# The second expert's weight loads take their number from the ranking, and the ranking stands ahead of the last table of slots

## The chip, the cores and the metric

The kernel runs on one core of one Trainium2 chip. The metric is the device time of one execution in microseconds (us), the median of several. Three executions of the kernel before took 1479.09, 1485.01 and 1486.35 us; their median is 1485.01 us. Another execution, taken with the profiler, lasted 1480.72 us, and its trace is what the sections below read.

## The reference

One decoder layer on 512 tokens of width 1024, in float32. A mixer (gated DeltaNet heads and sliding-window attention, one output projection) comes first, then a mixture of 32 experts of which each token takes 4. Cut to the second half, with its names:

```python
x = x + gate1 * (mixed @ w_out)
h = rmsnorm(x, norm2_w) * (1.0 + scale2) + shift2
logits = h @ w_router + b_router
top_val, top_idx = lax.top_k(logits, 4)
gates = jax.nn.softmax(top_val, axis=-1)
# for each token and each of its four experts e:
hu = h @ w_up[e] + b_up[e]
x_glu = jnp.minimum(hu[:, :1024], 7.0)
x_lin = jnp.clip(hu[:, 1024:], -7.0, 7.0)
act = x_glu * jax.nn.sigmoid(1.702 * x_glu) * (x_lin + 1.0)
out[token] += gates[token, e] * (act @ w_down[e] + b_down[e])
x = x + gate2 * out
```

An expert has 8 MB of `w_up` and 4 MB of `w_down`; all 32 are read, 384 MB in all.

## The kernel before

**The two stages.** The first stage (some 430 us) computes the mixer, the output projection in four tiles of 128 tokens, and for each tile its routing. The second runs through the 32 experts one after the other, in an order by rank: the experts are sorted by their number of tokens, and the program says which rank comes when and how many tokens a rank may hold. Which expert has a rank is known only at run time, from the ranking; only the expert at the first place (`ORDER[0]`) is fixed in the program. Its 12 weights of 1 MB (8 of `w_up`, 4 of `w_down`) are loaded during the first stage. The second expert is the first whose weights need the ranking.

**The routing of a tile** (`route`) is a chain over VectorE (DVE), TensorE (PE) and ScalarE (ACT): the residual `y` is added up (L1168, L1172), scaled (L1279), transposed (L1283), multiplied by the router (L1299 to L1306), and VectorE finds the four experts (L1311 to L1317, ending in the tile's counts `ohs`, L1316). TensorE then numbers the token within each expert (L1321, L1322), VectorE works out slot numbers (L1325 to L1331), and the table of slots is made: VectorE writes payload and selection (L1183, L1184, four L1192), TensorE multiplies them (L1196, four of them) and VectorE adds the product to `ten` (L1342).

**The ranking** (`ranks`) adds the counts of the four tiles on TensorE (L1504, L1506), compares each expert's count with all others on VectorE (L1508 to L1517, ending in a permutation), and multiplies the permutation on TensorE (L1521, L1522). ScalarE writes the result to `eri` (L1524): the expert number of each rank. `places` multiplies the finished `ten` by the permutation (L1535) and VectorE writes `gi` (L1537), the token numbers of each expert's slots.

**What sets the order.** In the first stage the instructions of all engines stand in the order that a planner (`Flow`) chooses while the program is built: every step is announced with an engine and a cost, and of the steps that can start at nearly the same time the one with the smallest priority number goes first. `PR["rt"]` is 4, so `ranks` is added with 3.9 and the routing of tile i with 4 - 0.2 i; the projection's end (`out_end`) and `finish` stand at 3. Each engine then runs its instructions strictly in that order.

**The start of the second stage.** SyncE's queue (SP) issues all weight loads. GpSimd (POOL) clears a tile `xg` (L1697) and gathers an expert's tokens into it by an indirect DMA (L1698) that reads `gi`; TensorE transposes them (L1711) and starts the up product (L1760). In the kernel before, POOL copies the second expert's number out of `eri` into a one-element tile `second` (L1904), and `behind` puts this copy after the issue of the first gather in POOL's order. SP reads `second` and issues the second expert's loads (L1654). There are 16 places of 1 MB for weights: the first expert holds 12, so the second expert's fifth load waits until TensorE is through with the first expert's first weight. After its sixth load (`THEN1`) SP issues the bias rows of both first experts (L1640); VectorE spreads them (L1720) before it can use any up product.

Of the kernel before, what the change touches and what calls it, by code (L numbers as in the profile page):

```python
# [12 lines left out]
I32 = mybir.dt.int32  # L13
# [12 lines left out]
NE = 32  # L26
# [12 lines left out]
PR = {"swa": 1, "conv": 5, "cend": 4, "in": 4, "late": 1, "z": 2, "load": 1, "yS": 7, "fin": 3, "rt": 4, "yT": 3, "rec": 1, "oout": 2}  # L39
# [10 lines left out]
ORDER = []  # L50
# [133 lines left out]
def layer_kernel(ctx: ExitStack, tc: tile.TileContext, A, out, probe=None):  # L184
    nc = tc.nc
    V, S, G, TE = nc.vector, nc.scalar, nc.gpsimd, nc.tensor
# [109 lines left out]
    def behind(late, early):  # L296

        tc.add_manual_dep(late.ins, early.ins.name,
                          mybir.DependencyInfo(mybir.DependencyClass.NoSync, mybir.DependencyReason.DATA), reason="order")
# [1197 lines left out]
    def ranks():  # L1497
        yield [("chosen", 2), ("oT", 7)]
        yield "N", 0.0, "d", "d"
        pa, pb = bank("d", "ps_cnt"), bank("d", "ps_cnt")  # L1500
        for i in range(NT):
            yield [("chosen", i)]
            yield "P", 0.2
            TE.matmul(pa[:, 0:NE], lhsT=bc(one, [P, P]), rhs=ohs[:, i], start=(i == 0), stop=(i == NT - 1))  # L1504
            for j in range(P // NE):
                TE.matmul(pb[NE * j:NE * j + NE, 0:1], lhsT=ohs[:, i], rhs=one, start=(i == 0), stop=(i == NT - 1))  # L1506
        yield "V", 0.4
        V.scalar_tensor_tensor(kr, pa[:, 0:NE], float(NE), C("KROW"), op0=OP.mult, op1=OP.add)  # L1508
        V.tensor_copy(ec[:, 1:2], pb[:, 0:1])
        V.scalar_tensor_tensor(ec[:, 0:1], ec[:, 1:2], float(NE), C("KCOL"), op0=OP.mult, op1=OP.add)  # L1510
        flow.give("d", "d")
        yield "V", 0.6
        V.tensor_scalar(kr, kr, ec[:, 0:1], None, op0=OP.is_gt)
        V.tensor_reduce(ec[:, 2:3], kr, axis=AX.X, op=OP.add)

        for c in range(2):
            V.tensor_scalar(ex[:, 1 + c], C("IOTA", 0, NE), ec[:, 2:3], C("ISC", c, c + 1), op0=OP.is_equal, op1=OP.mult)  # L1517
        flow.mark("perm")
        yield "P", 0.3, "d"
        pe = bank("d", "ps_er")  # L1520
        TE.matmul(pe[:NE, 0:NE], lhsT=bc(C("PIDX")[:NE], [NE, NE]), rhs=perm[:NE], start=True, stop=True)  # L1521
        TE.matmul(pe[:NE, NE:2 * NE], lhsT=bc(ec[:NE, 1:2], [NE, NE]), rhs=perm[:NE], start=True, stop=True)  # L1522
        yield "S", 0.5
        S.copy(eri, pe[:NE, 0:NE])  # L1524
        S.copy(cnti, pe[:NE, NE:2 * NE])
        S.copy(cnt[:NE], pe[:NE, NE:2 * NE])
        flow.give("d")
# [32 lines left out]
    with tc.manual_schedule(engines={nc.vector.engine, nc.scalar.engine, nc.tensor.engine, nc.gpsimd.engine, nc.sync.engine}):  # L1560
        columns(rows2, 32, 51)
        for i in range(NT):
            (V.tensor_copy if i % 2 else S.copy)(swt[i // 2][:, i % 2, 0:512], tq[i])
        for i in range(2):
            (V.tensor_copy if i % 2 else S.copy)(swt[i][:, :, 512:768], tkv[i].rearrange("p (i n) -> p i n", n=256))

        def chain(*tasks):
            for t in tasks:
                yield from t

        def swa():
            flow.add(PR["swa"], swa_norms())
            for i in range(NT):
                flow.add(PR["swa"], swa_heads(i))
                for kv in range(2):
                    flow.add(PR["swa"], swa_weights(i, kv))
                    flow.add(PR["swa"] - 1, swa_values(i, kv))
            yield [("norms",)]

        order = [(n, p, c0 + 256 * p) for p in range(2) for n, c0 in (("k", 512), ("q", 0), ("v", 1024))]  # L1580
        flow.add(1, gates())
        wins[512, 0] = wins[512, 1] = w0s
        for hf in range(2):
            flow.mark("win", 512, hf)
        flow.taken.update({"x": 2, "r": 1})
        flow.free["V"] = 1.9
        flow.add(0, chain(*(win(c0) for c0 in [c for _, _, c in order][1:] + [1536, 1536 + 256])))
        flow.add(PR["conv"], chain(*(conv(p, n, c0, PR["cend"]) for n, p, c0 in order)))
        for p in range(2):
            for f in (lengths, decay, turned, inverse, levels):  # L1590
                flow.add(PR["in"] + (f is levels), f(p))
        flow.add(PR["swa"], swa())
        flow.add(1, late_loads())
        flow.add(PR["late"], chain(*(late(r) for r in range(2, 6))))
        flow.add(PR["z"], chain(*(gate(p, PR["z"]) for p in range(2))))
        flow.add(PR["load"], loads())
        flow.add(PR["rec"], recur())
        for i in range(NT):
            flow.add(PR["yS"], out_swa(i))
            flow.add(PR["yT"], out_delta(i))  # L1600
            flow.add(PR["rt"] - 0.2 * i, route(i))
            if i < NT - 1:
                flow.add(PR["fin"], finish(i))
        flow.add(PR["rt"], router_bias())
        flow.add(PR["rt"] - 0.1, ranks())
        flow.add(0, places())
        flow.run()
    early.close()
# [265 lines left out]
        G.dma_start(lstd, lst)  # L1874

    down_of = {0: ahead[1]}
    second = const.tile([1, 1], I32, name="second")

    def fetch_up(q):

        r = ORDER[q]
        e = nc.sync.value_load(second if q == 1 else eri[0:1, r:r + 1], min_val=0, max_val=NE - 1)

        def then():
            for p in range(q) if q == 1 else ():
                load_bias(ORDER[p], NB[ORDER[p]], bias[p % 2])
            load_bias(e, NB[r], bias[q % 2])

        ws = weights_of(e)
        wu = load_up(ws[0], then, THEN if q > 1 else THEN1)  # L1890
        if q > 1:
            down_of[q - 1] = load_down(state["dn"])
        state["dn"] = ws[1]
        return wu
# [5 lines left out]
    overflow = overflow_list()  # L1900
    with tc.manual_schedule(engines={nc.sync.engine, nc.tensor.engine, nc.vector.engine, nc.scalar.engine}):
        xs = {0: rows_of(0)}

        behind(G.tensor_copy(second, eri[0:1, ORDER[1]:ORDER[1] + 1]), state["gather"])  # L1904
        ups = {0: ahead[0], 1: fetch_up(1)}
        xs[1] = rows_of(1)
        xT = {0: turn(xs.pop(0))}
        for d in stores[-2:]:
            behind(d, state["turned", 1])
        bbs = {0: spread_bias(NB[ORDER[0]], bias[0])}  # L1910
        acts, pend, last = {}, [], {}
        for q in range(NE + 1):
            if q < NE:
                r = ORDER[q]
                last[q] = None
                if len(units(NB[r])) > 1:
                    last[q] = units(NB[r])[-1], TE.value_load(cnti[0:1, r:r + 1], min_val=0, max_val=T)

                def turn_acts():
                    for p, u, l in pend:  # L1920
                        acts.setdefault(p, {})[u] = turn_act(u, l)
                    pend.clear()

                def turn_next():
                    if q + 1 < NE:
                        xT[q + 1] = turn(xs.pop(q + 1))
                    if q + 2 < NE:
                        xs[q + 2] = rows_of(q + 2)

                if 1 < q + 1 < NE:  # L1930
                    ups[q + 1] = fetch_up(q + 1)
                elif q + 1 == NE:
                    down_of[q] = load_down(state["dn"])
                for z, us in enumerate(passes(NB[r])):
                    pu = up_pass(us, ups[q], xT[q], {3: [turn_acts], 5: [turn_next] if z == 0 else []}, last[q])
                    for u in us:
                        pend.append((q, u, swiglu(u, pu[u], bbs[q])))
                xT.pop(q), ups.pop(q), bbs.pop(q)
            else:
                turn_acts()  # L1940

            if q >= OVQ:
                next(overflow, None)
            if q:
                r = ORDER[q - 1]
                us = units(NB[r])
                py = down(us, down_of.pop(q - 1), acts.pop(q - 1), last.pop(q - 1))
                for u in us:
                    put(u, py[u], si[u[1]][:, u[0] // 64, r:r + 1], sg[u[1]][:, u[0] // 64, r:r + 1])
            if q >= OVQ:  # L1950
                next(overflow, None)
            if q + 1 < NE:
                bbs[q + 1] = spread_bias(NB[ORDER[q + 1]], bias[(q + 1) % 2])
# [47 lines left out]
```

## Time and profile before

| | kernel before |
|---|---|
| median of three runs | 1485.01 us |
| the profiled execution: its time / its span | 1480.72 us / 1478.9 us |
| TensorE, VectorE, ScalarE, GpSimd busy | 1381.5, 563.8, 237.8, 261.1 us |
| weight loads of the experts | 384 of 1 MB |
| bytes moved by DMA | 476.16 MB |

All times below count from the span's start; the profiled execution is 1.8 us longer than its span. A "timeline" row gives the start, the length, the engine, the line, the operation with the tiles it writes and reads, its size and number, and in brackets how long the engine stood idle before it and what ended that. SPq is SyncE's queue, which issues DMAs; such a row's length is the issue alone, and where several issues are merged in one row, the time from the first to the last.

### The profile page before, as it was taken

Reading aid. Unit: us, or ns where it says so; the run is one execution under the profiler, and the core shown is the slowest. Engines: PE = TensorE matmul, PEld = TensorE weight load, DVE = VectorE, ACT = ScalarE, POOL = GpSimd, SP = SyncE. Lnnn points to the kernel's source line nnn. Section 1 sums busy time; section 2 is a strip of 40 time slices with the busy share of each in tenths; the row PEclk is TensorE's granted clock in tenths of the full one; section 3 lists DMA queues with packets and bytes.
Section 4 is the critical chain, followed back from the end, with each engine's and each line's share of the span. In section 5 each row is a group of like instructions: output and inputs, shape, how many; then the busy total and the mean of one; then the engine's idle time right before and its main releaser. Section 6 shows DMA issues by size and latency. Waiting matters only on the chain. (4 is left out here: it accounts for less than half of the span.)

```text
span 1478.9 us, 22303 instructions
## 1 busy us (share of the span) xinstructions
PE 1381.5 (93%) x8586; PEld 601.3 (41%) x8586; DVE 563.8 (38%) x1247; ACT 237.8 (16%) x542; POOL 261.1 (18%) x216
## 2 busy tenths in 40 slices
PE   4999999999879999979999999999999999999974
PEld 3766666765443333322333333333333333343311
DVE  6965567566853222212221231223321323232310
ACT  4354354442211000000000000000000000010000
POOL 2213133202331111101011101102110112211110
PEclk9999999999969999999999999999999999999976
DMA  9655300256349999999999999999998999999995
GB/s 302 212 200 204 113 29 30 58 214 277 116 152 407 409 387 402 396 391 412 411 412 400 379 419 394 384 409 393 410 367 349 403 348 404 393 418 415 414 415 229
DMA packets 104980, 476.16 MB, mean 322 GB/s; under 512 B 13992, under 2 KB 39556, under 8 KB 55714
## 3 DMA queue, kind: packets, MB, share of 16 engines
q1 hardware_dynamic: 91842, 453.16, 77.4%
q0 software_dynamic: 11952, 18.75, 5.5%
q10 hardware_dynamic: 1072, 2.70, 0.5%
q8 instruction: 75, 1.23, 0.3%
q14 instruction: 39, 0.32, 0.1%
HBM read 464.14 MB, written 17.22 MB: 325 GB/s over the span
## 5 line engine op out<-in xcount | busy, mean ns | idle before, releaser
L1760 PE MATMUL ps_up<-we,xTe 128*64 128x512 f32 (+1 forms) x3040 | 622.2, 607 | 21.2 <-DMA we<-in_w_up_dram 16.8
L1760 PEld LDWEIGHTS ps_up<-we,xTe 128*64 128x64 f32 (+1 forms) x3040 | 188.5, 132 | 394.2 <-issue 336.8
L1797 PE MATMUL ps_dn<-we,aT 128*64 128x512 f32 (+1 forms) x1848 | 316.0, 534 | 19.7 <-DMA we<-in_w_down_dram 10.9
L1797 PEld LDWEIGHTS ps_dn<-we,aT 128*64 128x64 f32 (+1 forms) x1848 | 103.7, 129 | 232.2 <-issue 187.2
L1805 POOL DMA_INDIRECT out_dram<-yv,si x52 | 81.7, 1571 | 649.7 <-DVE yv L1804 464.9
L1712 DVE COPY xTe<-ps_xTe 128x256 f32<-128x256 f32 (+3 forms) x35 | 17.5, 501 | 307.4 <-PE ps_xTe L1711 307.4
L1785 ACT COPY aT<-ps_aT 128x512 f32<-128x512 f32 (+1 forms) x52 | 26.0, 530 | 512.5 <-PE ps_aT L1783 509.1
L1769 DVE TENSOR_TENSOR hu<-ps_up,bb 128x512 f32<-128x512 f32 (+1 forms) x52 | 32.1, 617 | 198.8 <-PE ps_up L1760 198.8
L1804 DVE SCALAR_TENSOR_TENSOR yv<-ps_dn,sg,g2p 128x512 f32<-128x512 f32 x38 | 28.5, 751 | 188.3 <-PE ps_dn L1797 187.4
L1771 ACT ACTIVATE hu<-hu 128x512 f32<-128x512 f32 (+1 forms) x52 | 29.8, 573 | 269.4 <-DVE hu L1770 269.4
L1697 POOL MEMSET xg<- 64x1024 f32 (+3 forms) x35 | 37.2, 1084 | 186.0 <-PE ps_xTe L1711 185.8
L317 PE MATMUL ps_ch<-hhi,wih 128*128 128x512 f32 x128 | 58.5, 457 | 0.0
L317 PE MATMUL ps_ch<-hl,wih 128*128 128x512 f32 x128 | 50.8, 397 | 0.0
L317 PE MATMUL ps_ch<-hhi,wl 128*128 128x512 f32 x128 | 50.5, 395 | 0.0
L1720 DVE STREAM_SHUFFLE bb<-bias 128x1024 f32<-128x1024 f32 (+1 forms) x44 | 48.8, 1137 | 0.1
L1712 ACT COPY xTe<-ps_xTe 128x256 f32<-128x256 f32 (+3 forms) x35 | 15.1, 433 | 163.4 <-PE ps_xTe L1711 163.4
L1698 POOL DMA_INDIRECT xg<-h2d,gi x35 | 35.7, 1021 | 16.1 <-POOL xg L1697 8.1
L1711 PEld LDWEIGHTS ps_xTe<-cst,xg 64*128 64x128 f32 (+3 forms) x280 | 24.1, 142 | 32.3 <-issue 23.1
L1783 PEld LDWEIGHTS ps_aT<-cst,act 128*128 128x128 f32 x180 | 24.3, 208 | 28.6 <-issue 25.7
L1711 PE MATMUL ps_xTe<-cst,xg 64*128 64x64 f32 (+3 forms) x280 | 30.1, 249 | 5.1 <-DMA xg<-h2d,gi 2.2
L317 PEld LDWEIGHTS ps_ch<-hhi,wih 128*128 128x128 f32 x128 | 24.2, 189 | 23.2 <-issue 18.0
L1142 PE MATMUL ps_y<-wos,oS 128*128 128x512 f32 x64 | 33.3, 613 | 0.0
(392 smaller groups left out, 1389.0 us busy)
## 6 DMA issues: line engine op xcount, KB each, us to landing
we<-in_w_up_dram SPq DMA_DIRECT2D x256, 1024.0 KB
we<-in_w_down_dram SPq DMA_DIRECT2D x128, 1024.0 KB
wa<-in_w_ada_dram SPq DMA_DIRECT2D x16, 512.0 KB
wi<-in_w_in_dram SPq DMA_DIRECT2D x8, 1024.0 KB
wl<-in_w_ada_dram SPq DMA_DIRECT2D x12, 512.0 KB
oS<-in_w_ada_dram SPq DMA_DIRECT2D x10, 512.0 KB
LL<-in_w_ada_dram SPq DMA_DIRECT2D x10, 512.0 KB
wt<-in_w_in_dram SPq DMA_DIRECT2D x4, 776.0 KB
```

Of the source, the lines that this page charges most:

```text
L317: TE.matmul(acc, lhsT=w[a], rhs=x_[b], start=start and q == 0, stop=stop and q == 2)
L1142: TE.matmul(a, lhsT=oS[:, j, P * i:P * i + P], rhs=wo[j][:, 512 * hf:512 * hf + 512], start=(j == 0), stop=(j == 3))
L1697: G.memset(xg[:rows_], 0.0)
L1698: state["gather"] = G.indirect_dma_start(out=xg[:rows_], out_offset=None, in_=h2d, in_offset=bass.IndirectOffsetOnAxis(ap=gidx(g)[:rows_], ...
L1711: TE.transpose(pt[:, k, :rows_], xg[:rows_, 512 * hf + P * k:512 * hf + P * k + P], ident[:rows_, :rows_])
L1712: state["turned", hf] = (S.copy if hf else V.tensor_copy)(xt_[:, 4 * hf:4 * hf + 4, :rows_], pt[:, :, :rows_])
L1720: V.stream_shuffle(bbs[w].rearrange("p h n -> p (h n)"), b[w], [0] * 32)
L1760: TE.matmul(t[w * j:w * j + w], lhsT=lhsT, rhs=rhs, start=(k == 0), stop=(k == KT - 1))
L1769: V.tensor_tensor(g, pg, bbs[w][:, 0], op=OP.add)
L1771: S.activation(sgm, g, AF.Sigmoid, scale=1.702)
L1797: TE.matmul(py[u][w * j:w * j + w, 0:m], lhsT=aT[u][:, kt % nf, w * (kt // nf):w * (kt // nf) + w], rhs=wd[kt][:, m * j:m * j + m], start= ...
L1805: G.indirect_dma_start(out=outv[u[1]], out_offset=bass.IndirectOffsetOnAxis(ap=sidx, axis=0), in_=yv, in_offset=None, compute_op=OP.add, b ...
```

## The change

Two edits. The second expert's loads read their number from `eri` itself, as those of all later experts do: the tile `second`, POOL's copy and its place behind the first gather are gone. And `ranks` is added to the planner with priority 3 in place of 3.9.

```diff
-        flow.add(PR["rt"] - 0.1, ranks())
+        flow.add(PR["rt"] - 1, ranks())
...
-    second = const.tile([1, 1], I32, name="second")
...
-        e = nc.sync.value_load(second if q == 1 else eri[0:1, r:r + 1], min_val=0, max_val=NE - 1)
+        e = nc.sync.value_load(eri[0:1, r:r + 1], min_val=0, max_val=NE - 1)
...
-        behind(G.tensor_copy(second, eri[0:1, ORDER[1]:ORDER[1] + 1]), state["gather"])
```

The new priority changes the planner's order over some 30 us at the end of the first stage. Three places matter.

VectorE, the last tile, from its slot numbers to the sum of its gates. L1183 to L1192 are the table, L1513 to L1517 the ranking's second half. Before:

```order
L1331 TENSOR_SCALAR slots<-si_3884,cse 128x4
L1508 SCALAR_TENSOR_TENSOR ex<-ps_cnt,cse 128x32
L1509 COPY ec<-ps_cnt 128x1
L1510 SCALAR_TENSOR_TENSOR ec<-ec,cse 128x1
L1183 TENSOR_TENSOR rt<-kS,slots 128x4x32
L1184 TENSOR_TENSOR rt<-kS,slots 128x4x32
L1192 TENSOR_SCALAR room<-cst,slots 128x256 x4
L1513 TENSOR_SCALAR ex<-ex,ec 128x32
L1514 TENSOR_REDUCE ec<-ex 128x1
L1517 TENSOR_SCALAR ex<-cst,ec,cse 128x32 x2
L1338 TENSOR_REDUCE sums<-rt 128x32
```

The same place of the changed kernel:

```order
L1331 TENSOR_SCALAR slots<-si_3882,cse 128x4
L1373 TENSOR_TENSOR bt<-ps_bd,gm 128x512
L1513 TENSOR_SCALAR ex<-ex,ec 128x32
L1514 TENSOR_REDUCE ec<-ex 128x1
L1517 TENSOR_SCALAR ex<-cst,ec,cse 128x32 x2
L1183 TENSOR_TENSOR rt<-kS,slots 128x4x32
L1184 TENSOR_TENSOR rt<-kS,slots 128x4x32
L1192 TENSOR_SCALAR room<-cst,slots 128x256 x4
L1338 TENSOR_REDUCE sums<-rt 128x32
```

The ranking's second half now stands ahead of the table, and so does a product of the third tile's `finish` (L1373) that stood before the choice; L1508 to L1510 moved ahead of L1325, further up.

TensorE, the last tile, from its logits to the product that yields `eri`. Before:

```order
L1306 MATMUL ps_rt<-cst,rt 128x32 x2
L1321 MATMUL ps_rt<-sums,one 128x32 x3
L1322 MATMUL ps_rt<-sums,cse 128x32
L1504 MATMUL ps_cnt<-sums,one 128x32
L1506 MATMUL ps_cnt<-one,sums 32x1 x4
L1196 MATMUL ps_rt<-room,rt 64x256 x4
L1521 MATMUL ps_er<-ex,cst 32x32
```

The same place of the changed kernel:

```order
L1306 MATMUL ps_rt<-cst,rt 128x32 x2
L1504 MATMUL ps_cnt<-sums,one 128x32
L1506 MATMUL ps_cnt<-one,sums 32x1 x4
L1321 MATMUL ps_rt<-sums,one 128x32 x3
L1322 MATMUL ps_rt<-sums,cse 128x32
L1370 MATMUL ps_bd<-bdh,fin 128x512
L1196 MATMUL ps_rt<-room,rt 64x256 x4
L1521 MATMUL ps_er<-ex,cst 32x32
```

The last tile's count now stands ahead of its numbering, and L1521 still stands behind the table's four products.

TensorE, some 15 us earlier, around the third tile's table and the last tile's projection (L1161) and transposes (L1283). Before:

```order
L1161 MATMUL ps_y<-wod,oT 128x512
L1196 MATMUL ps_rt<-room,rt 64x256 x4
L1504 MATMUL ps_cnt<-sums,one 128x32
L1506 MATMUL ps_cnt<-one,sums 32x1 x4
L1161 MATMUL ps_y<-wod,oT 128x512
L1504 MATMUL ps_cnt<-sums,one 128x32
L1506 MATMUL ps_cnt<-one,sums 32x1 x4
L1161 MATMUL ps_y<-wod,oT 128x512
L1283 MATMUL ps_h2T<-cst,h_3811 128x128 x4
```

The same place of the changed kernel:

```order
L1504 MATMUL ps_cnt<-sums,one 128x32
L1506 MATMUL ps_cnt<-one,sums 32x1 x4
L1161 MATMUL ps_y<-wod,oT 128x512
L1283 MATMUL ps_h2T<-cst,h_3800 128x128 x4
L1161 MATMUL ps_y<-wod,oT 128x512
L1321 MATMUL ps_rt<-sums,one 128x32 x2
L1322 MATMUL ps_rt<-sums,cse 128x32
L1196 MATMUL ps_rt<-room,rt 64x256 x4
L1283 MATMUL ps_h2T<-cst,h_3800 128x128 x4
```

The third tile's numbering (L1321, L1322) and table (L1196) moved behind the projection's last products; before, they stood ahead of them.

## Rows read from the trace of the kernel before

**Rows 1.** Windows: us, busy per engine (instructions), clock, DMA share, GB/s.
```profile
420.00:431.50 11.50, 8.13 (x75) 5.87 (x75) 7.74 (x35) 1.49 (x8) 4.21 (x6) 0.50 0.10 27
431.50:441.00 9.50, 7.23 (x25) 3.00 (x24) 3.04 (x5) 0.58 (x1) 7.03 (x9) 0.62 0.89 275
460.00:1440.00 980.00, 947.57 (x5135) 328.77 (x5131) 263.22 (x530) 70.34 (x136) 139.25 (x113) 0.99 1.01 398
```

**Rows 2.** Waits of SyncE's queue: us in total, times, longest.
```profile
SPq L1882 <- POOL second L1904: 25.8, 1, 25.8
```

**Rows 3.** Timeline, from the ranking's result to the second expert's first load.
```profile
426.75 0.17 ACT L1524 CAST eri<-ps_er 32x32 int32<-32x32 f32 x1 [6.20 <-PE ps_er L1522]
429.13 1.10 POOL L1698 DMA_INDIRECT xg<-h2d,gi  x1 [7.12 <-issue]
430.23 0.18 POOL L1904 COPY second<-eri 1x1 int32<-1x1 int32 x1
431.47 0.37 SPq L1654 DMA_DIRECT2D we<-in_w_up_dram  x1
```

**Rows 4.** Timeline, last tile, VectorE and TensorE, from the choice to the ranking.
```profile
418.11 1.49 PE L1321 MATMUL ps_rt<-sums,one 128*128 128x32 f32 x6 [0.36 <-DVE rt L1311]
419.69 0.37 DVE L1316 TENSOR_REDUCE sums<-kS 128x32 f32<-128x128 f32 x1
420.17 1.85 POOL L1697 MEMSET xg<- 128x1024 f32 x2
420.56 0.61 PE L1504 MATMUL ps_cnt<-sums,one 128*128 128x32 f32 x2
420.78 1.26 DVE L1326 TENSOR_SCALAR slots<-rt 128x4 f32<-128x4 f32 x1
422.10 0.29 DVE L1328 TENSOR_REDUCE slots<-rt 128x4 f32<-128x128 f32 x1
423.73 1.13 DVE L1192 TENSOR_SCALAR room<-cst,slots 128x256 f32<-128x256 f32 x4
424.13 2.23 PE L1196 MATMUL ps_rt<-room,rt 128*64 128x256 f32 x8 [2.74 <-DVE room L1192]
424.78 0.23 DVE L1513 TENSOR_SCALAR ex<-ex,ec 128x32 f32<-128x32 f32 x1
425.27 0.51 DVE L1517 TENSOR_SCALAR ex<-cst,ec,cse 128x32 f32<-128x32 f32 x2
426.29 0.31 PE L1521 MATMUL ps_er<-ex,cst 32*32 32x32 f32 x2
```

**Rows 5.** Timeline, third tile's table and last projection.
```profile
401.91 1.02 PE L1161 MATMUL ps_y<-wod,oT 128*128 128x512 f32 x2
402.77 0.30 PE L1504 MATMUL ps_cnt<-sums,one 128*128 128x32 f32 x2
406.25 1.50 PE L1196 MATMUL ps_rt<-room,rt 128*64 128x256 f32 x8 [1.95 <-DVE room L1192]
412.45 0.69 DVE L1279 TENSOR_TENSOR h<-y,gm 128x512 f32<-128x512 f32 x1
```

**Rows 6.** Gathers (L1698): the first, the third, all 35, from issue to landing.
```profile
DMA to landing us min/median/max: 4.8/4.8/4.8
...
DMA to landing us min/median/max: 12.4/12.4/12.4
...
DMA to landing us min/median/max: 4.8/8.5/12.4
```

**Rows 7.** Timeline, the first expert's start.
```profile
435.85 5.09 PE L1760 MATMUL ps_up<-we,xTe 128*64 128x512 f32 x16
440.98 0.33 SPq L1654 DMA_DIRECT2D we<-in_w_up_dram  x1
457.10 0.01 DVE L1720 LOAD_MASK_SELECT bb<-bias  x1 [21.30 <-DMA bias<-in_b_up_dram]
458.77 7.07 PE L1760 MATMUL ps_up<-we,xTe 128*64 128x512 f32 x24 [2.37 <-DVE xTe L1712]
```

## The prediction

> **What bounds the kernel now.** I read the windows first, since the two stages have different limits. From 460 to 1440 us the DMA engines have a share of 1.01 at 398 GB/s, while TensorE is busy 947.57 of 980 us, so 32.4 us of it are idle [rows 1]. This stretch is bound by the stream of expert weights: it ends earlier only if the stream starts earlier or has fewer gaps. Before it, from 420 to 431.5, the DMA share is 0.10 at 27 GB/s, and from 431.5 to 441 it is 0.89 at 275 GB/s [rows 1]: the stream has not begun, then it ramps. The waits of SyncE's queue say why: once, for 25.8 us, it waits for `second` [rows 2]. So a microsecond by which the second expert's first load comes earlier is worth up to one at the end, and no more than the idle DMA time of that place.
>
> **What is removed.** The number stands in `eri` at 426.75 + 0.17 = 426.92. POOL issues the first gather at 429.13, copies from 430.23 to 430.41, and the first load is issued at 431.47 [rows 3]. The detour costs 430.41 - 426.92 = 3.49 us; the 1.06 us from number to issue stay. With `eri` where it is, the first load would come at 427.98, and 3.49 us is the gain at most from this edit.
>
> **What is moved, on the way to `eri`.** Two terms, with opposite signs.
>
> First, how early the last tile chooses its experts (L1316 ends at 420.06 [rows 4]). Before, TensorE stood 1.95 us for the third tile's table at 406.25 and then spent 1.50 on it, with two of the projection's products (0.86 each: 402.77 - 401.91) behind it [rows 5]. Now those products go first, up to 3.45 us earlier. But VectorE then has the third tile's slots and table ahead of the last tile's second half of L1279 (412.45 [rows 5]); the last tile's own slots and table took 424.86 - 422.10 = 2.76 [rows 4]. The bounds for this term are -3.45 (all of it gained, nothing in the way) and +2.76 (nothing gained); the net is -0.7, and since the third tile's table can run beside the last tile's transposes I take -1.0.
>
> Second, from the choice to `eri`. The last tile's numbering (L1321, 1.49) used to run on TensorE while VectorE was still choosing: it began at 418.11 [rows 4]. Now the count stands ahead of it and needs the choice, so the numbering comes after it: 0.50 until the count starts (420.56 - 420.06), 0.61 for L1504, about half of that for the narrow L1506, 1.49 for L1321 and a third of it for L1322 make 3.4 us. Before, L1328 began 2.04 us after the choice (422.10): +1.36. Ahead of the table come L1373 (a product of L1279's size, 0.69 [rows 5]) and L1513 to L1517 (424.78 to 425.78, 1.00 [rows 4]). L1508 to L1510 leave this stretch and fill the wait for the numbering, below L1513's 0.23 each [rows 4], together 0.4. That is 1.36 + 0.69 + 1.00 - 0.4 = +2.65 for the table. On TensorE L1521 stood directly behind the table's L1196 before (424.13 + 2.23 = 426.36, L1521 at 426.29 [rows 4]) and stands there still, so taking the ranking ahead of the table on VectorE gives `eri` nothing: it comes when the table is through. The bounds are 0 (the late numbering and the ranking hidden) and 2.65 + 1.85 = +4.5, if the two memsets (1.85 [rows 4]) fall upon the table. That they can is in the trace: L1326 took 1.26, against 0.23 for L1513, a like instruction, and it ended when the memsets did [rows 4]. I take +2.65, since the memsets already cost about 1 us before.
>
> [...]
>
> Together `eri` comes 1.65 later, at 428.6, the first load at 429.6, which is 1.84 earlier than 431.47. `gi` hangs on the same table, so the first gather is later by the same 1.65: 430.8.
>
> **What the gather meets.** Before, the first gather ran ahead of all weights and landed in 4.8 us; the third, issued behind four loads, took 12.4; the median of all 35 is 8.5 [rows 6]. Now up to four loads of 1 MB are issued from 429.6, ahead of the gather. Its latency lies between 4.8 and 12.4, and I take the median, as the third had two gathers before it too. It lands at 430.8 + 8.5 = 439.3 against 433.9, 5.4 us later, and TensorE starts the up product at 441.2 instead of 435.85 [rows 7].
>
> [...]
>
> **What then feeds the stream.** Four of the 16 places are free, so the fifth load waits for TensorE: it was issued at 440.98, 5.13 us after the up product began [rows 7], and now comes at 446.4. When are the first four through? By 441 some 275 x 9.5 = 2.6 MB had moved; the four loads (4.2 MB) and three gathers (128, 64 and 96 rows of 4 KB, 1.2 MB) are 5.4 MB, the other 2.8 at 398 GB/s need 7 us: 448, now 1.84 earlier, 446.2. The stream runs dry for about 0.2 us plus the ramp of a new load, which I estimate as the idle part of the first 9.5 us (0.11 x 9.5 = 1.0 [rows 1]): 1.2. Of 1.84 us, 0.6 stay. With a gather of 4.8 us there is no gap (-1.84); with 12.4 the gap is 5.1 and the sum is +3.3.
>
> What becomes late next on TensorE: it stands 2.37 us at 458.77, after VectorE had waited for the bias rows until 457.10 [rows 7]. SyncE issues these after the sixth load, so they shift with TensorE's start, but with fewer loads ahead of them; I let that stall go, which leaves TensorE about 3 us late. That costs nothing as long as the stream is the bound, since 32.4 us of idle time lie behind it [rows 1]; without that cover it costs the 3 us. POOL's copy, 0.18 us, leaves an engine that is idle most of the time: nothing.
>
> **Sum.** -1.84 + 1.2 = -0.6 us. The profiled execution took 1480.72, so 1480.1; it lies 4.3 us under the median of the three runs, and on that median the forecast is 1484.4 us.
>
> **The rivals.** (1) The loads start earlier and the gather is not held: for it speaks that the first gather needs only 4.8 us on empty engines and that the DMA share is 0.10 there; against it the third gather's 12.4. With `eri` where it was before, the gain is the whole detour, -3.5: 1481.5 on the median. (2) Slower: the late tokens starve the stream. Its place is the fifth load, which waits for TensorE's first weight; from a gather latency of about 8 us on it decides. At 12.4 TensorE starts 1.65 + 7.6 = 9.3 us late, the stream has lost 3.3 net, and if TensorE's lateness less the 2.4 of the bias stall is never recovered, the end is 6.9 later. I price it in the middle, +5: 1490.0. For it: 12.4 at the third gather; against: 32.4 us of idle TensorE. (3) The change doesn't do what it says: the ranking's result is not there earlier for SyncE than `second` was, since POOL's instructions fall upon the table. `eri` 3.5 us or more late: the stream starts where it did, the gather comes 3.5 to 4.5 later: +1 to +2, 1486.5.
>
> **How the numbers follow.** Forecast 0.50, rival 1 0.20, rival 2 0.18, rival 3 0.12. The forecast's own range is -2.5 to +2. Between the ends of all cases, -3.5 and +6.9, lie 1481.5 and 1491.9; the three runs spread from 5.9 under their median to 1.3 over it, and the median of the changed kernel will too. I leave out the last part of rival 2 and reach down for the spread: 1477.5 to 1490.5. About 0.5% (7.4 us) is what a measurement of this kernel can tell from no change. No case by itself gets there, and only the gain or loss of a case with the spread on top does: faster 0.09, within 0.83, slower 0.08.
>
> **What would show it.** In the profile after, SyncE's first load behind the ranking should stand near 429.6 and no wait for POOL's copy in its list; L1521 still directly behind L1196; the first gather near 430.8 with a latency near 8.5; the up product's start near 441; the fifth load near 446 with a short dip of the DMA share ahead of it. The prediction is wrong in its first term if the first load is earlier than 428 or later than 431.5, in its second if the gather lands in under 6 us, and as a whole if TensorE's late start shows as idle DMA time later than 470.

## The result, and the profile after

The changed kernel takes 1493.28 us (median of five runs, 1491.46 to 1494.29) where the kernel before, beside it on the same chip, takes 1485.01 (five runs, 1479.09 to 1486.35). The ratio is 1.0071, with a 95% interval from 1.0054 to 1.0088. It is slower by 8.3 us, and outside the predicted range. The profiled execution took 1494.10 us, its span is 1492.3.

The start of the second stage comes first, since the prediction rests on it. The timeline after, from the last tile's choice to the bias rows (columns as in [rows 3]):

```profile
417.49 0.37 DVE L1316 TENSOR_REDUCE sums<-kS 128x32 f32<-128x128 f32 x1
...
422.44 0.23 DVE L1513 TENSOR_SCALAR ex<-ex,ec 128x32 f32<-128x32 f32 x1
422.68 1.25 POOL L1377 TENSOR_TENSOR y<-y,bt 128x512 f32<-128x512 f32 x1 [5.19 <-DVE ex L1513]
422.92 1.25 DVE L1517 TENSOR_SCALAR ex<-cst,ec,cse 128x32 f32<-128x32 f32 x2
...
424.50 3.07 DVE L1192 TENSOR_SCALAR room<-cst,slots 128x256 f32<-128x256 f32 x4
424.78 1.86 POOL L1697 MEMSET xg<- 128x1024 f32 x2
...
426.84 2.22 PE L1196 MATMUL ps_rt<-room,rt 128*64 128x256 f32 x8 [5.65 <-DVE room L1192]
...
429.00 0.31 PE L1521 MATMUL ps_er<-ex,cst 32*32 32x32 f32 x2
...
429.45 0.17 ACT L1524 CAST eri<-ps_er 32x32 int32<-32x32 f32 x1 [11.11 <-PE ps_er L1522]
430.68 20.82 SPq L1654 DMA_DIRECT2D we<-in_w_up_dram  x6
431.84 1.10 POOL L1698 DMA_INDIRECT xg<-h2d,gi  x1 [5.20 <-issue]
...
441.32 1.97 PE L1711 MATMUL ps_xTe<-cst,xg 128*128 128x128 f32 x8 [7.67 <-DMA xg<-h2d,gi]
...
443.22 5.82 PE L1760 MATMUL ps_up<-we,xTe 128*64 128x512 f32 x16
...
451.97 2.74 SPq L1640 DMA_DIRECT2D bias<-in_b_up_dram  x4
...
456.91 0.01 DVE L1720 LOAD_MASK_SELECT bb<-bias  x1 [13.75 <-DMA bias<-in_b_up_dram]
```

Against [rows 3, 4, 7]: `eri` comes 2.70 later, the first load 0.79 earlier (430.68 for 431.47), the gather is issued 2.71 later, TensorE starts the up product 7.37 later. SyncE no longer waits for `second`. Its first waits now (the first is the wait for `eri`; the profile puts it down to ScalarE's L1365, a few instructions behind `eri`, but the first load follows the end of `eri` by 1.06 us, as it followed the end of the copy before):

```profile
SPq L1881 <- ACT fin L1365: 26.5, 1, 26.5
SPq L1654 <- PEq L1754: 13.3, 2, 12.5
```

The first three gathers meet the weights that now run ahead of them; from issue to landing (before 4.8 for the first and 12.4 for the third, [rows 6]):

```profile
DMA to landing us min/median/max: 9.4/10.3/11.1
```

So the start has the predicted order, with sizes that are partly off: the first load 0.8 us earlier and not 1.84, the up product 7.4 us later and not 5.4. The windows, which answer to [rows 1], show that this is not where the 8 us are. First one of the kernel before that [rows 1] lacks, then the changed kernel:

```profile
441.00:460.00 19.00, 16.09 (x76) 6.28 (x78) 2.86 (x6) 0.52 (x2) 1.96 (x2) 0.98 1.02 404
```

```profile
420.00:431.50 11.50, 5.85 (x37) 4.17 (x41) 8.08 (x21) 0.59 (x4) 3.67 (x4) 0.50 0.06 23
431.50:441.00 9.50, 2.15 (x34) 1.25 (x34) 3.79 (x11) 0.50 (x2) 4.05 (x4) 0.50 1.00 354
441.00:460.00 19.00, 18.07 (x76) 7.45 (x78) 2.33 (x4) 0.96 (x2) 6.64 (x8) 0.83 0.90 305
460.00:1440.00 980.00, 943.90 (x5125) 328.81 (x5121) 263.69 (x530) 70.03 (x135) 136.31 (x112) 0.99 1.01 394
```

From 431.5 to 441 more is moved than before (354 GB/s for 275), from 441 to 460 less (305 for 404). But from 460 to 1440 us, which no edit of the change touches, the stream runs at 394 GB/s where it ran at 398, **at the same DMA share of 1.01**. A wait lowers the share, as from 441 to 460, where the fifth load waits for TensorE until 449.09: 0.90 for 1.02. From 460 on the engines are as busy as before and move less: each packet takes longer, 322.9 ns for 320.1 on average by the packet records below. The issue times of the weight loads say the same (after minus before, us, from the two timelines; the loads are counted from 0, so load 12 is the second expert's first):

| load | 12 | 16 | 32 | 64 | 128 | 192 | 256 | 320 | 376 |
|---|---|---|---|---|---|---|---|---|---|
| after - before | -0.8 | +8.1 | +3.4 | +1.7 | +4.0 | +4.8 | +7.6 | +11.7 | +12.8 |

By load 64 the start has cost some 2 us, and then the gap widens over the rest of the stage, at the end to about what the two profiled executions differ by (1494.10 - 1480.72 = 13.4; that one of before was a short one).

What could reach every load of the stage? The tile `second` was also 32 bytes of SBUF per partition. The tiles above it in the left stack of pools moved down by 32 bytes when it went, and 13 of the 16 weight places are among them. Their addresses in the two built programs, and what is left over a multiple of 256:

```
                            before                 left over   after                  left over
13 weight tiles, left side  28416, 36608, 44800 ...        0   28384, 36576, 44768 ...      224
3 weight tiles, right side  159712, 212960, 221152       224   the same                     224
```

The duration of the 8192-byte packets (one partition's row of a weight tile) from 460 to 1440 us has a mean of 320.1 ns before and 322.9 after, and three quarters of them take at most 309 before and 319 after. From the second expert on there are 372 loads of 128 rows on 16 engines, 2976 packets each: 2976 x 2.8 ns = 8.3 us, an estimate. The packets are those of the two profiled executions, which differ by 13.4 us, so by this estimate they account for 8.3 of these; that the medians differ by 8.3 too is chance. Some 2 us of the rest are the start, and some 3 us stay without an account.

### The profile page after: what moved, and what is told of

The parts are those of the page before. It is cut to its first block, busy times and chain, and to the rows that moved or that the text cites. A ratio compares the mean times of both kernels' runs of the same rounds, so it can differ in the third digit from the quotient of the medians.

```text
span 1492.3 us, 22302 instructions
## 1 busy us (share of the span) xinstructions
PE 1380.5 (93%) x8586; PEld 600.3 (40%) x8586; DVE 565.1 (38%) x1247; ACT 237.6 (16%) x542; POOL 260.8 (17%) x215
## 5 line engine op out<-in xcount | busy, mean ns | idle before, releaser
L1698 POOL DMA_INDIRECT xg<-h2d,gi x35 | 35.4, 1012 | 14.4 <-POOL xg L1697 8.0
```

What stands on the lines that cost most here:

```text
L1698: state["gather"] = G.indirect_dma_start(out=xg[:rows_], out_offset=None, in_=h2d, in_offset=bass.IndirectOffsetOnAxis(ap=gidx(g)[:rows_], ...
```

## The experiments

Theory A: the addresses. Theory L, its rival: the order of loads and gather at the start. The kernel before ran beside all of them (its medians: 1482.16 for the first four, 1482.36 for the next four, 1482.04 for the last). The packet columns are worked out from the packet records as above.

| kernel | median us | ratio to before, 95% | GB/s 460 to 1440 | mean packet ns | 75% take at most, ns |
|---|---|---|---|---|---|
| the change | 1493.28 | 1.0071, 1.0054 to 1.0088 | 394 | 322.9 | 319 |
| e1, the change, addresses restored | 1482.84 | 1.0006, 0.9995 to 1.0017 | 398 | 319.5 | 309 |
| e2, before, 13 tiles +32 | 1490.86 | 1.0062, 1.0044 to 1.0081 | 394 | 322.8 | 319 |
| e5, before, 13 tiles +64 | 1489.76 | 1.0049, 1.0034 to 1.0063 | 394 | 322.3 | 316 |
| e12, before, 13 tiles +128 | 1487.59 | 1.0045, 1.0028 to 1.0062 | 396 | 321.3 | 316 |
| e6, before, 9 tiles +32 | 1488.09 | 1.0038, 1.0025 to 1.0050 | 395 | 321.5 | 314 |
| e8, before, all 16 on 256 | 1477.65 | 0.9964, 0.9951 to 0.9976 | 399 | 318.8 | 309 |
| e4, before, only the ranking moved | 1483.00 | 1.0007, 0.9995 to 1.0019 | 398 | 319.8 | 309 |
| e3, direct number only, addresses restored | 1477.44 | 0.9971, 0.9951 to 0.9990 | 398 | 320.1 | 309 |
| e9, the same kernel as e3 | 1480.51 | 0.9996, 0.9980 to 1.0011 | 399 | 319.7 | 309 |
| e7, e3 and all 16 on 256 | 1478.11 | 0.9963, 0.9950 to 0.9976 | 399 | 319.1 | 309 |
| e11, the change and all 16 on 256 | 1477.49 | 0.9972, 0.9958 to 0.9986 | 398 | 319.8 | 309 |
| e10, before, 16 on 256, pools reordered | 1487.94 | 1.0041, 1.0027 to 1.0055 | 398 | 319.8 | 309 |

**e1: the change with the old addresses.** A tile that stays is made 32 bytes wider; every instruction of the change stands.

```diff
-    ntot = const.tile([1, 1], I32, name="ntot")
+    ntot = const.tile([1, 9], I32, name="ntot")[:, 0:1]
```

> The changed kernel, with one small tile made 64 bytes wide in place of 32, so that the weight tiles lie again at the addresses of the kernel before (the removed tile had moved 13 of the 16 weight places down by 32 bytes, from multiples of 256 bytes to odd multiples of 32). Instructions and their order are those of the changed kernel. Theory A (the addresses): the weights' packets of 8192 bytes take 309 ns again in the median and not 313, the drift after 650 us (from +2 to +13 us in the issue of the loads) is gone, and the time is 1484 to 1488 us. Theory L (the late first gather and nothing else): 1491 to 1495 us, as the changed kernel, packets at 313 ns.

The loss is gone: 1482.84, ratio 1.0006. In e1's trace the start is the changed one, and the stream is the old one. Timeline, then the window from 460 to 1440 us:

```profile
428.25 0.18 ACT L1524 CAST eri<-ps_er 32x32 int32<-32x32 f32 x1 [11.11 <-PE ps_er L1522]
429.49 20.50 SPq L1654 DMA_DIRECT2D we<-in_w_up_dram  x6
430.63 1.10 POOL L1698 DMA_INDIRECT xg<-h2d,gi  x1 [5.19 <-issue]
...
440.00 1.97 PE L1711 MATMUL ps_xTe<-cst,xg 128*128 128x128 f32 x8 [7.55 <-DMA xg<-h2d,gi]
441.90 5.62 PE L1760 MATMUL ps_up<-we,xTe 128*64 128x512 f32 x16
```

```profile
460.00:1440.00 980.00, 949.33 (x5151) 329.94 (x5147) 264.57 (x532) 70.45 (x136) 139.30 (x113) 0.99 1.01 398
```

Its loads are issued 6.6 us later than before's at load 16, 0.9 earlier at load 64 and 0.2 later at load 376: the delay of load 16 is gone after some 30 loads, and no drift follows. e1 isolates the scheduling edits, and they are worth nothing measurable.

**e2: the kernel before with new addresses.** The same line of e1, put into the kernel before; nothing of the change is in it, and the 13 tiles lie 32 bytes higher (28448 for 28416).

> The kernel before, with the same small tile 64 bytes wide, which moves the same 13 weight places up by 32 bytes, off their multiples of 256. Instructions and order are those of the kernel before. Theory A (the addresses): 5 to 10 us slower than the kernel before, packets at 313 ns in the median, the start of the second stage unchanged (first load near 431.5, up product near 436). Theory L (the late first gather): no difference beyond 2 us, packets at 309 ns.

It takes 1490.86, ratio 1.0062. Its window has the changed kernel's 394 GB/s, again with a share of 1.01:

```profile
460.00:1440.00 980.00, 941.96 (x5107) 327.46 (x5103) 264.40 (x532) 70.01 (x135) 137.26 (x112) 0.99 1.01 394
```

The start, which was expected unchanged (431.5 and 436), is late in this profile:

```profile
435.20 12.31 SPq L1654 DMA_DIRECT2D we<-in_w_up_dram  x6
439.50 5.55 PE L1760 MATMUL ps_up<-we,xTe 128*64 128x512 f32 x16
```

TensorE's granted clock is 0.5 from 409.2 to 416.0, where the kernel before still has 1.0 until 414.9: two of the projection's products (L1161) take 2.07 us for 1.12. Of the 12.1 us between the profiled executions of e2 and of the kernel before, 3.3 are there at load 64, and 8.3 are added between loads 64 and 376, so the stream slows down in e2 as in the changed kernel, and part of e2's loss may be the start.

e1 and e2 together settle the cause of the loss: the addresses alone bring it (e2), and without them it isn't there (e1). The cleanest pair is the change and e1, whose starts are alike and which differ by the 32 bytes alone.

**e5 and e12: which boundary.** `[1, 17]` and `[1, 33]` in place of `[1, 9]` shift the 13 tiles by 64 and 128 bytes. In e12 five small tiles of the last loop (over late experts, which runs no round here) stand in dead columns of `gi` and `slots`, to make room.

> The kernel before, with the number of late experts in a tile of 17 columns instead of 1, so that everything that lies above it in SBUF, 13 of the 16 weight tiles among it, begins 64 bytes higher (28480 for 28416, and so on); nothing else differs. Moving the same 13 tiles by 32 bytes cost 8.7 us (1490.86 against 1482.16). Theory A256, only tiles that begin at a multiple of 256 bytes are filled at full speed: the same again, +8 to +9 us, the steady stage from 460 to 1440 us at 394 GB/s, the median packet of 8192 bytes at 313 ns. Rival A64, a multiple of 64 bytes is enough: 0 within 1.5 us, 398 GB/s, 309 ns. Between the two, +3 to +6: the cost follows the distance from a boundary.

> The kernel before with the same 13 weight tiles 128 bytes higher (28544 for 28416, and so on), the five small tiles of the loop over late experts put into dead columns to make room; the three on the right stay 32 below a multiple of 256. Shifts of 32 and 64 bytes gave 1.0062 and 1.0049. Theory A256, only a multiple of 256 counts: +7 to +9 us, ratio 1.005 to 1.006, 394 GB/s. Rival A128, a multiple of 128 is enough: 1.000 within 0.001, 398 GB/s. A cost that shrinks with the shift would show as 1.002 to 1.004.

Both are slower, by 7.4 and 5.5 us. A multiple of 64 or of 128 bytes is therefore not enough. (28416, the first place of the kernel before, is 111 times 256 and no multiple of 512, and 75% of that kernel's packets take at most 309 ns. Whether a multiple of 512 would be better no run shows.) The windows of e5 and of e12:

```profile
460.00:1440.00 980.00, 945.00 (x5111) 328.65 (x5111) 265.17 (x534) 70.00 (x135) 137.69 (x112) 0.99 1.01 394
```

```profile
460.00:1440.00 980.00, 943.53 (x5125) 327.94 (x5121) 264.86 (x534) 70.09 (x135) 137.97 (x112) 0.99 1.01 396
```

The cost does not grow with the distance from the boundary: 224 bytes past it (the change) cost 8.3 us, 32 cost 8.7, 64 cost 7.4 and 128 cost 5.5; the intervals of the last three overlap. That 128 costs less than the others is likely, since it is below the 7 to 9 us that theory A256 expected and its packets are less slow: 321.3 ns on average against 322.3 to 322.9, and 32% of them at 310 to 322 ns against 42 to 45% (table at the end of this section). With 13 rows of 16 moved, the mean packet is longer than before's by 0.8% at 32 bytes past the boundary, 0.7% at 64, 0.4% at 128 and 0.9% at 224. What a packet past the boundary does in that time no run shows.

**e6: nine tiles of 13.** An unused tile of 32 bytes is allocated between the fourth and the fifth weight place, so that only those above it move.

```diff
+    ctx.enter_context(tc.tile_pool(name="odd", bufs=1)).tile([P, 8], F32, name="odd")
     ring2 = ctx.enter_context(tc.tile_pool(name="ring2", bufs=RING2, reuse_waits="tile"))
```

> The kernel before with an unused tile of 32 bytes between the fourth and the fifth weight tile: nine of the 16 weight tiles begin 32 bytes higher, the other seven stay. Theory of shares, each load pays for its own tile: 9 of 13 times 8.7 is +6.0 us (ratio 1.004), 395 GB/s. Rival, the cost comes from a few of the 13 tiles or from the work that lies in the first four (the gather ring of the routing): 0 to +2 us. Rival, one misplaced tile holds up all: +8 to +9 us.

+5.7 us, where shares gave +6.0; the interval (0.25 to 0.50%) excludes both rivals. That the size fits so well is partly luck: in e6's profile the first load is 5.0 us late, as in e2 with TensorE's clock at 0.5 ahead of it, and only 3.7 us are added between loads 64 and 376, against 8.3 in e2. That each load pays for its own tile is borne out better by the packets: those of 310 to 322 ns are 5% before, 28% with nine tiles moved and 44% with 13. The price of one tile stays uncertain.

**e3, e9 and e4: the scheduling edits one by one.** e3 is e1 with the ranking's priority put back, so that only the direct number is left; e9 is the same kernel once more. e4 is the kernel before with the new priority alone.

> Only the second expert's number straight from the ranking, with the old priority of the ranking and the addresses of the kernel before. Theory L: the first load comes at 428.0, the gather is issued at 429.1 as before and lands 9 us later (9.4 in the changed kernel) and not 4.8, so the up product starts 4 to 5 us later than 435.85; the time is 0 to 4 us over the kernel before. Rival (the earlier loads are worth their 3.5 us): 2 to 3.5 us under the kernel before.

> Only the ranking's priority, the number still read from the tile that POOL copies behind the first gather; addresses are those of the kernel before. Theory L: number, gather and first load are all about 2.7 us later than before, the gather lands in under 5.5 us, the up product starts 2.5 to 3 us later, and the time is 2 to 3.5 us over the kernel before. Rival (the order of the first stage costs nothing by itself): no difference beyond 1 us. Theory A: no more than that, packets at 309 ns.

> The second expert's number straight from the ranking, ranking in its old place, the 13 weight tiles at their old addresses: the same kernel that gave -4.7 us (0.9971, from 0.9951 to 0.9990) once more, because the same edit on top of 16 aligned tiles gave nothing (1478.11 with it, 1477.65 without). If the gain is real and tied to the three unaligned tiles on the right: 0.997 again. If it was chance: between 0.9985 and 1.001, near the -0.6 us of the forecast for the whole change.

The direct number measured -4.7 us the first time and -1.5, with 1 inside the interval, the second. Both intervals together allow 1.5 to 3 us, and e7 against e8 below shows none, so the 4.7 was chance in part, and what the edit is worth stays open. Moving the ranking costs nothing that can be told from none (1.0007), though `eri` comes 1.4 us later in e4's profile; theory L had expected +2 to +3.5. Its timeline shows why the ranking came late, here too:

```profile
423.17 3.07 DVE L1192 TENSOR_SCALAR room<-cst,slots 128x256 f32<-128x256 f32 x4
423.45 1.86 POOL L1697 MEMSET xg<- 128x1024 f32 x2
...
428.13 0.17 ACT L1524 CAST eri<-ps_er 32x32 int32<-32x32 f32 x1 [11.11 <-PE ps_er L1522]
```

The same `eri` in e3's, with the old priority, and its loads ahead of the gather:

```profile
426.60 0.17 ACT L1524 CAST eri<-ps_er 32x32 int32<-32x32 f32 x1 [6.20 <-PE ps_er L1522]
...
427.83 19.49 SPq L1654 DMA_DIRECT2D we<-in_w_up_dram  x6
428.98 1.10 POOL L1698 DMA_INDIRECT xg<-h2d,gi  x1 [7.12 <-issue]
```

**e8, e7 and e11: the other three tiles too.** The three weight places on the right lay 32 bytes below a multiple of 256 in the kernel before. An unused tile of 224 bytes above them moves them, and all else on the right side, onto one; the room is made as in e12.

```diff
+    room_for("even").tile([P, 56], F32, name="even")
     ringo, hup, actp, moe, aTp, ringy, moel, misc = (room_for(n) for n in ("ringo", "hu", "act", "moe", "aT", "ringy", "moel", "misc"))
```

> The kernel before with the three weight tiles on the right side moved down by 224 bytes, so that all 16 begin at a multiple of 256 (an unused tile of 224 bytes above them; the room comes from five small tiles of the loop over late experts, put into dead columns of two tables; that loop runs no round here). Theory of shares: three more of 16 loads pay no toll, 3 of 13 times 8.7 is 2.0 us, so -2.0 (ratio 0.9986, which five rounds can just tell from 1), 399 to 400 GB/s from 460 to 1440 us. Rival, the right three pay nothing now, since only the distance of 32 bytes counts and they lie 32 bytes below a boundary, or since they fill while others do: 0 within 1 us.

> The second expert's number straight from the ranking, the ranking in its old place, the 13 weight tiles at their old addresses (this much measured -4.7 us, ratio 0.9971), and the three weight tiles on the right at multiples of 256 as well. If the two gains add up: -4.7 - 2.0 = -6.7 us, ratio 0.9955, some 1476 us where the kernel before takes 1482.5. Rival, the right three don't matter: -4.7 us again, ratio 0.997. Rival, the -4.7 was partly chance, as the theory of the loads' order gave at most -3.5: ratio 0.998 to 0.9975 with the right three at nothing.

> The changed kernel whole, with the ranking ahead of the last tile's table too, and every weight tile and gather tile at a multiple of 256. If the scheduling edits are worth nothing, as they were with 13 aligned tiles (1482.84 against 1482.16): as the kernel before so aligned, ratio 0.9964, some 1477.5 us. If the later ranking costs what its 1.7 us say: 0.9975.

All three beat both kernels: 1477.65 (the kernel before so aligned), 1478.11 (with the direct number) and 1477.49 (with both edits), 4.3 to 4.7 us under the kernel before beside them, where the change was 8.3 over it. No difference between the three is larger than their intervals; e11's ratio leaves open whether the later ranking costs 1 to 2 us. The gain is larger than the 2.0 that three shares give. The gathered rows (`xg`) and the scattered ones (`yv`) moved onto the boundary too, and the right-hand tiles now lie upon other tiles of the first stage, so the start differs too: in e11 POOL's clearing of `xg` waits for TensorE and so keeps clear of the table. Its timeline:

```profile
424.94 1.16 DVE L1192 TENSOR_SCALAR room<-cst,slots 128x256 f32<-128x256 f32 x4
427.72 1.83 POOL L1698 MEMSET xg<- 128x1024 f32 x2 [2.49 <-PE ps_rt L1196]
427.99 0.17 ACT L1524 CAST eri<-ps_er 32x32 int32<-32x32 f32 x1 [9.20 <-PE ps_er L1522]
```

**e10: which of them brings the rest.** Another order of the right side's pools, so that the weight tiles (and the small tiles of `misc`, with the bias rows) stand on 256, and `xg` and `yv` do not.

```diff
+    hup, actp, moe, aTp, moel = (room_for(n) for n in ("hu", "act", "moe", "aT", "moel"))
+    room_for("even").tile([P, 56], F32, name="even")
+    ringo, ringy, misc = (room_for(n) for n in ("ringo", "ringy", "misc"))
-    ringo, hup, actp, moe, aTp, ringy, moel, misc = (room_for(n) for n in ("ringo", "hu", "act", "moe", "aT", "ringy", "moel", "misc"))
```

> The kernel before with the three weight tiles on the right at multiples of 256 and all other tiles on the right (gathered rows, their transposes, the rows that are scattered) still 32 below one; the right side's pools are opened in another order for it. Both were moved together in the kernel that took 1477.65 against 1482.36 (ratio 0.9964). Theory of shares: the weight tiles alone bring -2.0 us (0.9986), and the gathered and scattered rows the other 2.7. Rival, all of it is the weight tiles, 1.6 us each: 0.9964 again. Rival, the weight tiles bring nothing, all of it is the gathers and scatters: 1.000.

None of the three: +5.9 us. The reason is the start, so the time answers another question. Its second gather tile now shares room with tiles of the projection's end, and POOL clears it only when VectorE is through with them; the loads follow 6.6 us after before's. POOL and SyncE:

```profile
422.77 0.97 POOL L1699 MEMSET xg<- 128x1024 f32 x1
434.45 0.94 POOL L1699 MEMSET xg<- 64x1024 f32 x1 [10.72 <-DVE bt L1373]
435.57 1.10 POOL L1700 DMA_INDIRECT xg<-h2d,gi  x1 [0.17 <-POOL xg L1699]
...
438.11 17.35 SPq L1654 DMA_DIRECT2D we<-in_w_up_dram  x6
```

From load 32 (+9.2) to load 376 (+8.7) it loses nothing more, at 398 GB/s.

**Start and stream apart, in all runs.** The issue times of the loads, less those of the kernel before, in us (one profiled execution of each kernel), and the share of the 8192-byte packets from 460 to 1440 us that take 310 to 322 ns, where 309 is the commonest duration in every run:

| kernel | load 12 | load 64 | load 376 | 64 to 376 | 310 to 322 ns |
|---|---|---|---|---|---|
| before | 0 | 0 | 0 | 0 | 5% |
| e1, e3, e4, e9: its addresses | -4.5 to +1.4 | -4.7 to -0.7 | -4.4 to +0.2 | -0.2 to +1.1 | 5% |
| the change | -0.8 | +1.7 | +12.8 | +11.0 | 45% |
| e2, 13 tiles +32 | +3.7 | +3.3 | +11.6 | +8.3 | 44% |
| e5, 13 tiles +64 | +1.6 | +1.5 | +8.6 | +7.1 | 42% |
| e12, 13 tiles +128 | +3.5 | +2.8 | +7.3 | +4.5 | 32% |
| e6, 9 tiles +32 | +5.0 | +5.3 | +9.0 | +3.7 | 28% |
| e8, all on 256 | +4.1 | -1.4 | -3.4 | -2.0 | 1% |
| e7, e11, all on 256 | +1.9 to +4.4 | -1.1 to -0.2 | -3.0 to -1.8 | -1.9 to -1.6 | 1% |
| e10, weight tiles on 256 | +6.6 | +9.6 | +8.7 | -0.9 | 1% |

The share of slow packets follows the number of misplaced weight tiles (it is smaller at 128 bytes than at 32, 64 or 224), and e10 has it as low as e8, so the weight tiles alone bring it. In e8 some 2.0 us come from the stream behind load 64, which is what three shares gave; what brings the rest of its 4.7 stays open. So does what makes TensorE's clock fall early (to 0.5 for 6.8 us, from between 404.8 and 409.2 on) in e2, e5, e6, e7, e8, e10 and e12, which have the old order of the ranking and moved tiles, and not in the kernel before, e3 and e9, which have the old addresses.

## Why the prediction was wrong

**The step that failed** is the last of its sum: the copy that is removed "leaves an engine that is idle most of the time: nothing". It priced the instruction and not its destination. Behind it stands the premise of the first paragraph, that the stretch "ends earlier only if the stream starts earlier or has fewer gaps", which took the stream's speed as given. The tile `second` held up the place of 13 weight tiles; without it the rows of the weights took 0.9% longer on average (322.9 ns for 320.1), an estimate of 8.3 us in all by the packets. e1, with the place restored and every instruction of the change kept, has no loss left that can be told from none (-0.7 to +2.5 us), and e2 loses 8.7 us by addresses alone. None of the three rivals contained it. Rival 2 came near the time (1490.0) by another cause: it asked for a stream that starves, and where the loads waited for TensorE, from 441 to 460 us, the DMA share was 0.90, not the 1.01 of the stretch from 460 to 1440 us.

**The rest of the sum is not contradicted, in part by luck.** The forecast for the scheduling was -0.6 us; e1 measured a ratio of 1.0006, from 0.9995 to 1.0017 (-0.7 to +2.5 us), so the forecast lies at the end of the interval, and two errors of opposite sign in its steps partly cancel:

- *The choice earlier*: taken as -1.0 with -3.45 as the end, measured -2.20 (L1316 ends at 417.86, before 420.06), and -3.40 in e1, which has the same instructions.
- *From the choice to `eri`*: taken as +2.65 with +4.5 as the end, measured 11.59 against 6.69, +4.90, past that end. The term was too small by the instructions of POOL: the two memsets fell upon L1192 (3.07 us for 1.13), and L1377 upon L1517 (1.25 for 0.51). The prediction named this end and judged it the less likely one. Net, `eri` came 2.70 later, between the forecast's 1.65 and the third rival's 3.5, and 1.50 later in e1.
- *The loads*: 1.06 us from number to issue, as taken (429.62 to 430.68); L1521 directly behind L1196, as said.
- *The gather*: latency 9.4, taken as 8.5. It was held when loads in another queue were issued ahead of it (from 430.68, the gather at 431.84), as the third gather's 12.4 had suggested, and it did not land in the 4.8 us that rival 1 needed.
- *The fifth load*: 449.09, and 447.57 in e1 (load 16: +6.6), where 446.4 was said. The dip of the DMA share is there (0.90 from 441 to 460), and so is the end of the bias stall. The late TensorE then cost nothing that lasts, as said: e1 is level at load 376.

That the stream is the bound was read rightly. What was missing is the second half of that reading: what bounds the kernel must also be asked for its speed while it runs, and an edit reaches that by whatever moves its buffers.

## What to carry to other kernels

A tile that is added, removed or resized moves every tile allocated after it; where a stream of transfers bounds the kernel, compare the addresses of its buffers before and after, to a multiple of 256 bytes, before pricing anything else: here the kernels with 13 of 16 weight tiles moved off it were 5.5 to 8.7 us slower. When a stretch is slower at the same DMA share, look at what one packet takes and not for a wait (here 322.9 ns for 320.1, at 1.01). And large tiles that DMAs fill belong on such a boundary to begin with: here, three of 16 and their neighbours were off it in a tuned kernel, and putting them right was worth 4.3 to 4.7 us, some 2 of them in the stream.

## What the runs showed of the hardware

- Filling SBUF rows of 8192 bytes costs 318.8 to 319.8 ns a packet on average when all 16 weight tiles start at a multiple of 256 bytes (e7, e8, e10, e11), and 322.8 when 13 of them start 32 bytes past one and the rest 224 past (e2). Packets of 310 to 322 ns are 1% in the first case and 44% in the second; the share of the DMA engines stays at 1.01.
- A gather issued 1.2 us after the first of four 1 MB loads in another queue landed after 9.4 us, against 4.8 with no load ahead of it.
- Four VectorE instructions of 0.35 us each (L1192, 1.13 together before) took 3.07 us together, one of them 2.29, when two GpSimd memsets ran beside them in the changed kernel, and 1.16 where the memsets came later (e11).
